# Four list tables, one for each block of tokens, in place of one in a mixture-of-experts encoder block

## The chip, the core and the metric

The kernel is one program on one core of a Trainium2 chip. Its time is the device time of one execution in microseconds (us). Five engines run their own instruction streams and meet at semaphores: TensorE (PE, matrix products; its loads of stationary operands are listed as PEld), VectorE (DVE), ScalarE (ACT), GpSimd (POOL) and SyncE (SP, which here only issues transfers). Sixteen DMA engines move data between the device memory and the on-chip memory; SP and POOL issue nearly all transfers.

## What is computed

A block of an encoder for 512 tokens of width 1024: a layer norm, a token mixer (gated linear attention and differential attention), a layer norm, a mixture of 32 experts of which every token uses 4, and a last layer norm. What matters here is how tokens come to experts:

```
logits = xf @ router_w + router_b          # 512 x 32
top_v, top_i = top_k(logits, 4)            # 4 experts of each token
gates = softmax(top_v)
...                                        # tokens grouped by expert
g = min(xe @ w_gate[e] + b_gate[e], 7);  u = clip(xe @ w_up[e] + b_up[e], -7, 7)
a = g * sigmoid(1.702 g) * (u + 1);      yb = a @ w_down[e] + b_down[e]
y[token] += yb * gate
```

Each expert has three matrices of 1024 x 1024 float32, 4 MB each, so the experts read 403 MB of weights.

## The kernel before

The first 700 us or so compute the mixer, with its weights streamed through a ring of buffers. Then come the experts, one after the other in `experts`. The loop step `e` computes gate and up of expert `e` (`gate_up`), then down of expert `e - 1` (`down`). Their weights arrive in pieces of 1 MB, two rows of 128 x 1024, into twelve buffers; `load` issues the next piece on SP's queue as soon as a buffer is given back. Experts 0 to 3 are computed in three float32r products (high and low parts; ACT makes `wh`, DVE makes `wl`), the rest are sorted by their number of tokens and most are computed in plain float32 in 32-column pieces (L1334).

Work on the side is put between the k steps of these products through hooks and generators. `order` (step 0, up, k = 6 until step 1) sorts the experts and at its end writes a table in device memory, `s_tab`: one row of 512 entries for each expert place, of which entry *n* says which (token, choice) is the *n*-th of that expert. A token chooses four experts, there are four blocks of 128 tokens, so this is sixteen scatters by indirect DMA from POOL (L1698), each writing 128 numbers of 4 bytes, one for each token of a block. Sixteen scatters write one tensor, and the framework makes each of them wait until the one before it has landed. After them POOL makes the small matrices `R` (L1703), scales a row block of `z` (L1513), gathers the rows of a later expert into `x` (L1215), and at the end of step 1 reads the first 160 columns of the table back into `tab` (L1517); then it scatters expert 0's result (L1223).

`lists` runs in step 2 between the k steps of gate: it transposes `tab` on PE (L1710, L1711), copies it on ACT (L1714, L1715), spreads it by small products (L1718 to L1721) and turns it into row numbers on DVE. These row numbers serve the gathers and scatters of the experts from 4 on. PE executes its instructions in the order in which they are written, so L1710 stands between the products of k = 0 and k = 1 of gate in step 2, and whatever it waits for stops these products as well.

Also in step 1, `plan_rest` (L1491) loads the sorted order of the 28 later experts into SP's registers, between two transfers of weights.

Of the kernel before, what the change touches and what calls it, by code (L numbers as in the profile page):

```python
# [5 lines left out]
F32 = mybir.dt.float32  # L6
# [8 lines left out]
P = 128  # L15
T = 512
NB = T // P
D = 1024
KC = D // P
E = 32  # L20
# [8 lines left out]
WIDE = 20  # L29
# [99 lines left out]
class Weights:  # L129
# [3 lines left out]
    def __init__(self, tc, ring, raw, ahead=2):  # L133
        self.tc, self.ring, self.raw, self.ahead = tc, ring, raw, ahead
        self.todo, self.raws, self.subs = [], {}, []
        self.n_raw = self.n_sub = self.n_out = 0
        self.low = tc.nc.vector
# [756 lines left out]
class Moe:  # L894
# [5 lines left out]
    def __init__(self, tc, K, a, z, gr):  # L900
        nc, c = tc.nc, K.c
        self.tc, self.nc, self.K, self.c, self.a, self.z = tc, nc, K, c, a, z
        self.rp = rp = K.open("route", "right")

        self.raw_r = K.open("rawr", "right")
        self.head = self.raw_r.tile([P, RAW_K, D], F32, tag=f"raw{RAW_R}", bufs=1, name="head")
        self.rw = rp.tile([P, KC, E], F32, name="rw")
        self.rb = rp.tile([P, 1, E], F32, name="rb")
        nc.sync.dma_start(self.rw, a["router_w"][0].rearrange("(k p) e -> p k e", p=P))
        nc.sync.dma_start(self.rb[:, 0], a["router_b"].broadcast_to([P, E]))  # L910
        self.hT, self.picks, self.gr = {}, {}, gr
        self.lg = rp.tile([P, NB, E], F32, name="lg")
        self.mx = rp.tile([P, NB, 8], F32, name="mx8")
        self.ix = rp.tile([P, NB, 8], U32, name="ix8")
        self.gates = rp.tile([P, NB, 4], F32, name="gates")

        self.prg = rp.tile([P, NB, 3, E], F32, name="prg")
        self.pm, self.rv, self.gv = (self.prg[:, :, i] for i in range(3))
        self.sel = rp.tile([P, NB, E], F32, name="sel")
        self.picks[0] = rp.tile([P, NB, P], F32, tag="pick0", bufs=1, name="pick0")  # L920

        self.srow, self.grow = (rp.tile([P, N_FIXED], I32, name=n) for n in ("srow", "grow"))
        self.srows, self.grows = (rp.tile([P, 5 * E + 1], I32, name=n) for n in ("srows", "grows"))
        self.tab = rp.tile([E, TAB], F32, name="tab")
        nc.gpsimd.memset(self.tab, 0.0)
        self.d_tab = K.d_tab.rearrange("(s r) o -> s (r o)", r=T)[:, :TAB]
        nc.gpsimd.dma_start(self.d_tab, self.tab)

        self.oh = rp.tile([P, E], F32R, name="oh")
        for i in range(0, P, E):  # L930
            nc.vector.tensor_copy(self.oh[i:i + E], c.ident[i:i + E, i:i + E])
        self.ohs = rp.tile([P, 2, E], F32R, name="ohs")
        self.spread(0, E)
        self.bias = rp.tile([P, 3, T], F32R, name="bias")
        self.bias_parts = []

        bts = self.head.rearrange("p r (n t) -> p (r n) t", t=T)
        for which, n in enumerate(("exp_b_gate", "exp_b_up", "exp_b_down")):
            bt = bts[:, which]
            for i in range(4):  # L940
                nc.sync.dma_start(bt[i * E:(i + 1) * E], a[n][0][:, (i // 2) * T:(i // 2 + 1) * T])

            def parts(bt=bt, which=which):
                bias = self.bias[:, which]
                if which == 1:
                    nc.vector.tensor_scalar(bt, bt, 1.0, None, op0=ALU.add)
                nc.scalar.copy(bias, bt)
                for lo in (E, 3 * E):
                    nc.vector.tensor_sub(bias[lo:lo + E], bt[lo:lo + E], bias[lo:lo + E].bitcast(F32))
            self.bias_parts.append(parts)  # L950

        self.todo, self.kinds, self.keep, self.raws, self.subs = [], [], [], {}, []
        self.n_sub = self.n_out = self.n_split = 0
        self.ohg = {}

        self.n_raw = self.spare = len(SPARE)
        self.sub_pool = None
        self.n_w = 3 * KC // RAW_K * E
        for i in range(N_FIXED):
            self.plan(i, [])  # L960
        own = [(self.raw_r, f"raw{i}", 1) for i in range(RAW_R + 1)]
        self.free = own[:-1] + [(K.raw, "raw", RAW_BUFS)] * RAW_BUFS + own[-1:]
        self.slots, self.held, self.want, self.due = {}, [], 0, []
# [453 lines left out]
    def experts(self, out):  # L1417
        nc, c, tc, a = self.nc, self.c, self.tc, self.a
# [30 lines left out]
        for e in range(E):  # L1449
# [6 lines left out]
            def first(which, k):  # L1456
# [22 lines left out]
                if e == 2 and which == 0:  # L1479
                    next(lists, None)  # L1480
# [19 lines left out]
            def middle(k):  # L1500
                nonlocal xT
                self.tick()
                if rest and k in (K_U2 if WIDE <= e < WIDE + 2 else K_U):
                    rest.pop(0)()
                if k in K_X and 0 < e < E - 1:
                    if k == K_X[0]:
                        xT = self.place("x", FORM[e + 1])
                    self.turn_part(x, xT, FORM[e + 1], K_X.index(k))
                if k == 6 and e == 0:
                    for j, n in enumerate(("ln2_g", "ln2_b")):  # L1510
                        nc.sync.dma_start(self.K.gb[:, j], a[n].broadcast_to([P, D]))
                if k == 3 and e < NB:
                    nc.gpsimd.tensor_scalar_mul(self.z[e], self.z[e], ALPHA)  # L1513
                if k == 7 and e + 1 < E and (FORM[e + 1] is not None or e + 1 == WIDE):
                    self.biases_of(e + 1, FORM[e + 1] or SECOND)
                if k == 7 and e == 1:
                    nc.gpsimd.dma_start(self.tab, self.d_tab)  # L1517
                if k == 5:
                    if e + 2 < E:
                        self.gather(x, e + 2, FORM[e + 2])  # L1520
                    if e + 2 == WIDE:
                        nc.gpsimd.memset(x2[0], 0.0)
                        self.gather(x2[0], E, SECOND)
                    if e + 3 == WIDE:
                        wide.append(self.held.pop())
                        t = self.other(wide[0], F32, "x2").rearrange("p i (n t) -> p (i n) t", t=T)
                        x2.extend(t[:, i] for i in range(4))
# [83 lines left out]
    def order(self):  # L1611
# [3 lines left out]
        nc, c, rp, lt = self.nc, self.c, self.rp, self.left  # L1615
# [37 lines left out]
        pt = self.psl()  # L1653
# [5 lines left out]
        pl = self.psl()  # L1659
# [7 lines left out]
        pt = self.psl()  # L1667
        for b in range(NB):
            nc.tensor.matmul(pt[:, b * 3 * E:(b + 1) * 3 * E], lhsT=tr[:3 * E, b * P:(b + 1) * P],
                             rhs=bd[:3 * E].rearrange("p i e -> p (i e)"), start=True, stop=True)  # L1670
# [4 lines left out]
        pl = self.psl()  # L1675
# [18 lines left out]
        to = rp.tile([P, NB, 4], I32, name="to")  # L1694
        with nc.allow_low_precision(reason="whole numbers below 2^24"):
            nc.vector.tensor_reduce(to, eq, axis=AX.X, op=ALU.add)
        for i in range(4 * NB):
            nc.gpsimd.indirect_dma_start(out=self.K.d_tab, out_offset=bass.IndirectOffsetOnAxis(ap=to[:, i // 4, i % 4:i % 4 + 1], axis=0),  # L1698
                                         in_=c.val[:, i:i + 1], in_offset=None, bounds_check=E * T - 1, oob_is_err=False)

        R = self.R = lt.tile([P, NB, P], F32, tag="pe", bufs=2, name="R")
        for i, (g, lo) in enumerate(((2, 0), (4, 0), (4, 32), (4, 64))):
# [3 lines left out]
    def lists(self):  # L1706

        nc, c, rp = self.nc, self.c, self.rp
        pt = self.psl()
        nc.tensor.transpose(pt[:, :E], self.tab[:, :P], c.ident[:E, :E])  # L1710
        nc.tensor.transpose(pt[:E, E:2 * E], self.tab[:, P:], c.ident[:E, :E])  # L1711
        yield
        lt = self.left.tile([P, 2, E], F32, name="lt")
        nc.scalar.copy(lt[:, 0], pt[:, :E])  # L1714
        nc.scalar.copy(lt[:E, 1], pt[:E, E:2 * E])  # L1715
        yield
        pl = self.psl()
        nc.tensor.matmul(pl[:, :E], lhsT=c.ident, rhs=lt[:, 0], start=True, stop=True)  # L1718
        for i in range(4):
            nc.tensor.matmul(pl[:, (i + 1) * E:(i + 2) * E], lhsT=self.R[:, i], rhs=lt[:, 0], start=True, stop=True)  # L1720
        nc.tensor.matmul(pl[:, 5 * E:5 * E + 1], lhsT=self.R[:E, 1], rhs=lt[:E, 1, WIDE:WIDE + 1], start=True, stop=True)  # L1721
        yield
        n = 5 * E + 1
        r = self.left.tile([P, D], F32, tag="y", bufs=1, name="r")
        t, r = r[:, :n], r[:, T:T + n]
# [8 lines left out]
        w, h, f = slice(0, E), slice(E, 2 * E), slice(2 * E, n)  # L1734
# [137 lines left out]
TAB = P + 32  # L1872
# [4 lines left out]
def build(tc, a, out):  # L1877
    nc = tc.nc
    K = Ctx()
    K.c = c = Ctx()  # L1880
    dr = lambda n, s: nc.dram_tensor(n, s, F32).ap()
# [10 lines left out]

    K.open, K.close = open_pool, close_pool
    K.d_h1 = dr("s_h1", (T, D))
    K.d_tab = dr("s_tab", (E * T, 1))
    for n in ("oT", "rg", "sA", "sB", "mA", "bT"):
        setattr(K, "d_" + n, dr("s_" + n, (KC, P, T)))
    with tc.tile_pool(name="cst", bufs=1) as cp, \
            tc.tile_pool(name="psB", bufs=4, space=PSUM) as psB, tc.tile_pool(name="psL", bufs=4, space=PSUM) as psL:
        K.psB, K.psL = psB, psL  # L1900
        tab = cp.tile([P, C_MIX], F32, name="tab")
# [81 lines left out]
```

## Time and profile before

| | |
|---|---|
| median of three runs | 1884.68 us (1884.49 to 1887.01) |
| the profiled execution | 1889.02 us, of which its span 1887.2 us |
| PE busy | 1754.7 us, 93% of the span |
| DVE, ACT, POOL busy | 763.7, 621.6, 462.6 us |
| bytes moved | 524.92 MB, mean 278 GB/s |
| longest wait of PE for a DMA | 44.5 us, once, at L1710 |

Times in the rows are from the start of the span. A row of the view of waits says which engine at which line and tile waited for whom, how long in total, how often, and the longest. In a timeline a row has its start, its length, engine, line, operation, output and inputs, and in brackets how long the engine was idle before and what ended that. A window row lists the busy time of each engine in a stretch (with its instructions in brackets), the granted clock of PE as a share of full speed, the share of the DMA engines' time that was busy, and GB/s.

### The profile page before, as it was taken

Reading aid. Unit: us, or ns where it says so; the run is one execution under the profiler, and the core shown is the slowest. Engines: PE = TensorE matmul, PEld = TensorE weight load, DVE = VectorE, ACT = ScalarE, POOL = GpSimd, SP = SyncE. Lnnn points to the kernel's source line nnn. Section 1 sums busy time; section 2 is a strip of 40 time slices with the busy share of each in tenths; the row PEclk is TensorE's granted clock in tenths of the full one; section 3 lists DMA queues with packets and bytes.
Section 4 is the critical chain, followed back from the end, with each engine's and each line's share of the span. In section 5 each row is a group of like instructions: output and inputs, shape, how many; then the busy total and the mean of one; then the engine's idle time right before and its main releaser. Section 6 shows DMA issues by size and latency. Waiting matters only on the chain. (4 is left out here: it accounts for less than half of the span.)

```text
span 1887.2 us, 33795 instructions
## 1 busy us (share of the span) xinstructions
PE 1754.7 (93%) x14065; PEld 1179.7 (63%) x14065; DVE 763.7 (40%) x1104; ACT 621.6 (33%) x997; POOL 462.6 (25%) x381
## 2 busy tenths in 40 slices
PE   7899999999999999918999999999999999997996
PEld 5687887777777888817655555555555455542573
DVE  5346658766753457927720000000002410000488
ACT  5433345555552234716621011110103311100473
POOL 4203316744432126231111111111102010101104
PEclk9998999999999998969999999999999999999998
DMA  7233432124335774736999999999999999999992
GB/s 244 90 100 103 154 101 89 53 78 161 113 129 205 269 287 161 272 156 248 350 405 377 420 371 423 380 417 390 401 376 413 366 380 423 424 424 426 426 426 95
DMA packets 111458, 524.92 MB, mean 278 GB/s; under 512 B 15390, under 2 KB 15734, under 8 KB 61508
## 3 DMA queue, kind: packets, MB, share of 16 engines
q1 hardware_dynamic: 97940, 492.05, 66.9%
q0 software_dynamic: 11056, 26.47, 3.7%
q10 hardware_dynamic: 2304, 4.20, 0.6%
q8 instruction: 112, 1.84, 0.4%
q14 instruction: 46, 0.38, 0.1%
HBM read 490.72 MB, written 37.91 MB: 280 GB/s over the span
## 5 line engine op out<-in xcount | busy, mean ns | idle before, releaser
L1334 PE MATMUL psb<-raw,xn 128*32 128x256 f32 (+1 forms) x5952 | 438.9, 404 | 12.3 <-DMA raw<-in_exp_w_up_dram 7.7
L1334 PEld LDWEIGHTS psb<-raw,xn 128*32 128x32 f32 (+1 forms) x5952 | 206.5, 113 | 199.9 <-issue 61.6
L1350 DVE TENSOR_SCALAR u<-psb 128x512 f32<-128x512 f32 (+1 forms) x52 | 31.5, 605 | 619.0 <-PE psb L1334 619.0
L1046 DVE TENSOR_TENSOR wl<-raw,wh 128x1024 fp32r<-128x1024 f32 x162 | 194.4, 1222 | 102.4 <-issue 50.3
L1334 PE MATMUL psl<-raw,an 128*32 128x256 f32 (+1 forms) x2976 | 226.1, 402 | 3.2 <-DMA raw<-in_exp_w_down_dram 2.2
L1035 ACT CAST wh<-raw 128x1024 fp32r<-128x1024 f32 x162 | 167.8, 1050 | 80.9 <-PE psb L1325 41.6
L1215 POOL DMA_INDIRECT x<-s_h,grows x55 | 59.7, 1085 | 472.3 <-PE psl L1261 411.3
L228 PE MATMUL psb<-hTh,wh 128*128 128x512 f32 x384 | 162.6, 423 | 8.8 <-ACT sg L543 3.9
L1334 PEld LDWEIGHTS psl<-raw,an 128*32 128x32 f32 (+1 forms) x2976 | 105.9, 112 | 91.4 <-issue 34.0
L230 PE MATMUL psb<-hTl,wh 128*128 128x512 f32 x384 | 154.2, 402 | 0.0
L229 PE MATMUL psb<-hTh,wl 128*128 128x512 f32 x384 | 154.1, 401 | 0.0
L168 ACT CAST wh<-raw 128x1024 fp32r<-128x1024 f32 x88 | 91.8, 1046 | 129.2 <-PE psb L230 81.0
L1223 POOL DMA_INDIRECT s_y<-y,srows x52 | 52.8, 1015 | 317.5 <-ACT y L1413 161.0
L1262 ACT COPY xn<-psl 128x512 f32<-128x512 f32 (+1 forms) x38 | 18.8, 495 | 310.3 <-PE psl L1261 310.3
L169 POOL TENSOR_TENSOR wl<-raw,wh 128x1024 fp32r<-128x1024 f32 x36 | 91.7, 2548 | 113.7 <-ACT wh L168 76.5
L169 DVE TENSOR_TENSOR wl<-raw,wh 128x1024 fp32r<-128x1024 f32 x52 | 68.2, 1315 | 93.4 <-ACT wh L168 93.4
L1326 PE MATMUL psb<-wl,xh 128*128 128x512 f32 x224 | 90.1, 402 | 4.6 <-DVE wl L1046 4.5
L1324 PE MATMUL psb<-wh,xh 128*128 128x512 f32 x224 | 93.1, 415 | 1.0 <-ACT wh L1035 1.0
L228 PEld LDWEIGHTS psb<-hTh,wh 128*128 128x128 f32 x384 | 74.0, 193 | 28.2 <-ACT sg L543 4.8
L1325 PE MATMUL psb<-wh,xl 128*128 128x512 f32 x224 | 89.4, 399 | 0.7 <-DVE xl L1285 0.7
L230 PEld LDWEIGHTS psb<-hTl,wh 128*128 128x128 f32 x384 | 73.7, 192 | 18.8 <-DVE hTl L348 0.9
L229 PEld LDWEIGHTS psb<-hTh,wl 128*128 128x128 f32 x384 | 74.0, 193 | 18.1 <-issue 2.2
(453 smaller groups left out, 2773.9 us busy)
## 6 DMA issues: line engine op xcount, KB each, us to landing
raw<-in_exp_w_up_dram SPq DMA_DIRECT2D x128, 1024.0 KB
raw<-in_exp_w_down_dram SPq DMA_DIRECT2D x128, 1024.0 KB
raw<-in_exp_w_gate_dram SPq DMA_DIRECT2D x125, 1024.0 KB
raw<-in_w_in_dram SPq DMA_DIRECT2D x32, 1024.0 KB
s_y<-zero SPq DMA_DIRECT2D x16, 512.0 KB
raw<-s_y SPq DMA_DIRECT2D x8, 1024.0 KB
raw<-in_w_br_gla_dram SPq DMA_DIRECT2D x4, 1024.0 KB
raw<-in_w_br_diff_dram SPq DMA_DIRECT2D x4, 1024.0 KB
```

The lines of the kernel that those rows point to most:

```text
L168: nc.scalar.copy(h, raw[:, 2 * s:2 * s + 2])
L169: self.low.tensor_sub(l, raw[:, 2 * s:2 * s + 2], h.bitcast(F32))
L228: nc.tensor.matmul(out, lhsT=sh, rhs=mh, start=first, stop=False)
L229: nc.tensor.matmul(out, lhsT=sl, rhs=mh, start=False, stop=False)
L230: nc.tensor.matmul(out, lhsT=sh, rhs=ml, start=False, stop=last)
L1035: nc.scalar.copy(h, src)
L1046: nc.vector.tensor_sub(sub[2], sub[0], sub[1].bitcast(F32))
L1215: self.nc.gpsimd.indirect_dma_start(out=x[:, t * D // n:(t + 1) * D // n], out_offset=None, in_=self.K.d_h1.rearrange("t (n d) -> (t n) d" ...
L1324: nc.tensor.matmul(ps[n], lhsT=xh[:, k], rhs=h[:, cs], start=False, stop=False)
L1325: nc.tensor.matmul(ps[n], lhsT=xl[:, k], rhs=h[:, cs], start=False, stop=False)
L1326: nc.tensor.matmul(ps[n], lhsT=xh[:, k], rhs=l[:, cs], start=False, stop=k == KC - 1)
L1334: nc.tensor.matmul(ps[t * d // T][i * m:i * m + m, t * d % T:t * d % T + d], lhsT=xT[:, o:o + m], rhs=w[:, i * d:(i + 1) * d], start=False ...
```

## The change

There are four tables in device memory, `s_tab0` to `s_tab3`, one for each block of 128 tokens, in place of one. All four are cleared early, from a corner of `prg` instead of `tab`. The scatters go around the blocks: choice 0 of blocks 0, 1, 2, 3, then choice 1, and so on. The read-back at the end of step 1 becomes eight loads: of each table the first 128 columns of all 32 rows (`tab`), and for the one wide expert's row the 32 columns behind (`ext`). In `lists` the sum of the four tables and its transposition are made by four products with the identity that add up in one PSUM tile, and a fifth sums `ext` with ones. The later products are the same, with the second part narrowed to one column.

```diff
-        self.tab = rp.tile([E, TAB], F32, name="tab")
-        nc.gpsimd.memset(self.tab, 0.0)
-        self.d_tab = K.d_tab.rearrange("(s r) o -> s (r o)", r=T)[:, :TAB]
-        nc.gpsimd.dma_start(self.d_tab, self.tab)
+        self.d_tabs = [t.rearrange("(s r) o -> s (r o)", r=T)[:, :TAB] for t in K.d_tabs]
+        none = self.prg.rearrange("p b i e -> p (b i e)")[:E, :TAB]
+        nc.gpsimd.memset(none, 0.0)
+        for t in self.d_tabs:
+            nc.gpsimd.dma_start(t, none)
...
                 if k == 7 and e == 1:
-                    nc.gpsimd.dma_start(self.tab, self.d_tab)
+                    self.tab = left.tile([P, NB, P], F32, tag="pe", bufs=2, name="tab")[:E]
+                    self.ext = left.tile([NB, TAB - P], F32, name="ext")
+                    for b, t in enumerate(self.d_tabs):
+                        nc.gpsimd.dma_start(self.tab[:, b], t[:, :P])
+                        nc.gpsimd.dma_start(self.ext[b:b + 1], t[WIDE:WIDE + 1, P:])
...
-        for i in range(4 * NB):
-            nc.gpsimd.indirect_dma_start(out=self.K.d_tab, out_offset=bass.IndirectOffsetOnAxis(ap=to[:, i // 4, i % 4:i % 4 + 1], axis=0),
-                                         in_=c.val[:, i:i + 1], in_offset=None, bounds_check=E * T - 1, oob_is_err=False)
+        for j in range(4):
+            for b in range(NB):
+                nc.gpsimd.indirect_dma_start(out=self.K.d_tabs[b], out_offset=bass.IndirectOffsetOnAxis(ap=to[:, b, j:j + 1], axis=0),
+                                             in_=c.val[:, 4 * b + j:4 * b + j + 1], in_offset=None, bounds_check=E * T - 1,
+                                             oob_is_err=False)
...
-        nc.tensor.transpose(pt[:, :E], self.tab[:, :P], c.ident[:E, :E])
-        nc.tensor.transpose(pt[:E, E:2 * E], self.tab[:, P:], c.ident[:E, :E])
+        for b in range(NB):
+            nc.tensor.matmul(pt[:, :E], lhsT=self.tab[:, b], rhs=c.ident[:E, :E], start=b == 0, stop=b == NB - 1)
+        nc.tensor.matmul(pt[:E, E:E + 1], lhsT=self.ext, rhs=c.ones[:NB, 0:1], start=True, stop=True)
         yield
-        lt = self.left.tile([P, 2, E], F32, name="lt")
-        nc.scalar.copy(lt[:, 0], pt[:, :E])
-        nc.scalar.copy(lt[:E, 1], pt[:E, E:2 * E])
+        lt = self.left.tile([P, E + 1], F32, name="lt")
+        nc.scalar.copy(lt[:, :E], pt[:, :E])
+        nc.scalar.copy(lt[:E, E:], pt[:E, E:E + 1])
...
-    K.d_tab = dr("s_tab", (E * T, 1))
+    K.d_tabs = [dr(f"s_tab{b}", (E * T, 1)) for b in range(NB)]
```

On POOL, at the end of `order` in step 1, the kernel before has these instructions in a row (`z0`, `z1` are row blocks of the residual, `s_h1` holds the normalized tokens, `to` the places to write, `li` the list of overfull experts, `x` the rows of the next expert, `y` a result):

```order
L1513 TENSOR_SCALAR z0_4743<-z0_4743 128x1024
L1215 DMA x_5681<-s_h1,grow_5065 128x1024
L1698 DMA s_tab<-tab_64,to_6063 16384x1 x16
L1703 COPY R_6113<-tab_64 128x128 x4
L1496 TENSOR_LOAD li_6037
L1513 TENSOR_SCALAR z1_4744<-z1_4744 128x1024
L1215 DMA x_5681<-s_h1,grow_5065 128x1024
L1517 DMA tab_5068<-s_tab 32x160
L1223 DMA s_y<-y_6633,srow_5064 2048x1024
```

In the changed kernel the scatters stand at the same place and begin like this:

```order
L1217 DMA x_5683<-s_h1,grow_5065 128x1024
L1705 DMA s_tab0<-tab_64,to_6065 16384x1
L1705 DMA s_tab1<-tab_64,to_6065 16384x1
L1705 DMA s_tab2<-tab_64,to_6065 16384x1
L1705 DMA s_tab3<-tab_64,to_6065 16384x1
L1705 DMA s_tab0<-tab_64,to_6065 16384x1
```

and behind the sixteen scatters and the four copies of `R` POOL has:

```order
L1515 TENSOR_SCALAR z1_4744<-z1_4744 128x1024
L1217 DMA x_5683<-s_h1,grow_5065 128x1024
L1522 DMA tab_6620<-s_tab0 32x128
L1523 DMA ext_6621<-s_tab0 1x16x2
L1522 DMA tab_6620<-s_tab1 32x128
L1523 DMA ext_6621<-s_tab1 1x16x2
L1522 DMA tab_6620<-s_tab2 32x128
L1523 DMA ext_6621<-s_tab2 1x16x2
L1522 DMA tab_6620<-s_tab3 32x128
L1523 DMA ext_6621<-s_tab3 1x16x2
L1225 DMA s_y<-y_6644,srow_5064 2048x1024
```

A scatter now has the one to the same table four instructions ahead of it, not one; all other instructions of POOL keep their order, with eight loads where one was. Beside the tensors that it touches, the framework gives POOL's transfers eight semaphores in rotation, so a transfer also waits until the eighth before it has landed; of the eight loads this adds a wait to the last one only, for the gather into `x` ahead of them.

On PE, the products of gate in step 2 (`wh`, `wl` are the parts of the weights, `xh`, `xl` those of the tokens) are interrupted by `lists` here, in the kernel before:

```order
L1325 MATMUL psb<-wh,xl 128x512
L1326 MATMUL psb<-wl,xh 128x512
L1710 MATMUL psl<-tab 128x32
L1711 MATMUL psl<-tab 32x32
L1324 MATMUL psb<-wh,xh 128x512
```

and in the changed kernel here:

```order
L1327 MATMUL psb<-wh,xl 128x512
L1328 MATMUL psb<-wl,xh 128x512
L1719 MATMUL psl<-tab 128x32 x4
L1720 MATMUL psl<-ones,ext 32x1
L1326 MATMUL psb<-wh,xh 128x512
```

The place among the products is the same; the two transpositions, which waited for one load, are five small products, which wait for eight.

## Rows read from the trace of the kernel before

**Rows 1.** The page's first part: busy us, share of the span, instructions.
```profile
PE 1754.7 (93%) x14065; PEld 1179.7 (63%) x14065; DVE 763.7 (40%) x1104; ACT 621.6 (33%) x997; POOL 462.6 (25%) x381
```

**Rows 2.** Waits of all engines: who for whom, us in total, times, longest.
```profile
PE psl L1710 <- DMA tab<-s_tab: 44.5, 1, 44.5
POOL s_tab L1698 <- DMA s_tab<-tab,to: 44.0, 15, 5.6
```

**Rows 3.** Windows: busy PE, PEld, DVE, ACT, POOL; clock; DMA share; GB/s.
```profile
784.00:812.00 28.00, 25.95 (x116) 20.59 (x114) 26.67 (x27) 21.37 (x24) 9.28 (x7) 1.00 0.49 177
812.00:854.00 42.00, 0.00 (x0) 0.00 (x0) 0.62 (x1) 0.00 (x0) 16.23 (x18) 0.52 0.41 162
854.00:858.00 4.00, 3.48 (x10) 2.74 (x11) 0.19 (x1) 0.93 (x3) 1.82 (x1) 0.50 0.06 24
1000.00:1600.00 600.00, 599.21 (x7592) 320.33 (x7590) 66.62 (x90) 90.30 (x166) 81.58 (x80) 1.00 0.98 395
```

**Rows 4.** Timeline of PE around its longest wait.
```profile
809.65 0.39 PE L1326 MATMUL psb<-wl,xh 128*128 128x512 f32 x1
...
854.52 0.28 PE L1710 MATMUL psl<-tab 32*128 32x32 f32 x1 [44.48 <-DMA tab<-s_tab]
```

**Rows 5.** Timeline of POOL: scatters 1, 2, 3, 8, 9, 16 and what follows.
```profile
783.77 1.75 POOL L1698 DMA_INDIRECT s_tab<-tab,to  x1 [10.46 <-DVE to L1696]
787.60 1.90 POOL L1698 DMA_INDIRECT s_tab<-tab,to  x1 [2.08 <-DMA s_tab<-tab,to]
794.49 0.97 POOL L1698 DMA_INDIRECT s_tab<-tab,to  x1 [5.00 <-DMA s_tab<-tab,to]
...
815.45 0.97 POOL L1698 DMA_INDIRECT s_tab<-tab,to  x1 [5.58 <-DMA s_tab<-tab,to]
821.69 0.98 POOL L1698 DMA_INDIRECT s_tab<-tab,to  x1 [5.27 <-DMA s_tab<-tab,to]
...
845.04 0.98 POOL L1698 DMA_INDIRECT s_tab<-tab,to  x1 [1.91 <-DMA s_tab<-tab,to]
846.02 0.99 POOL L1703 COPY R<-tab 128x128 f32<-128x128 f32 x4
...
849.94 1.09 POOL L1215 DMA_INDIRECT x<-s_h,grow  x1 [0.18 <-issue]
851.04 0.59 POOL L1517 DMA_DIRECT2D tab<-s_tab  x1
```

**Rows 6.** Groups of POOL's instructions, 783 to 812: busy us, mean ns.
```profile
L1698 POOL DMA_INDIRECT s_tab<-tab,to x7 | 9.5, 1358 | 27.1 <-DMA s_tab<-tab,to 16.6 <-DVE to L1696 10.5
```

**Rows 7.** Timeline of POOL, 921 to 926: gathers of one expert.
```profile
921.61 1.54 POOL L1215 DMA_INDIRECT x<-s_h,grows  x1 [23.03 <-PE psl L1261]
923.46 1.50 POOL L1215 DMA_INDIRECT x<-s_h,grows  x1 [0.31 <-issue]
```

**Rows 8.** The gathers' line, 840 to 1000: issue to landing.
```profile
DMA to landing us min/median/max: 5.8/6.1/6.4
```

**Rows 9.** Timeline of DVE, 784 to 812: its longest stretch without a pause.
```profile
785.13 11.95 DVE L1046 TENSOR_TENSOR wl<-raw,wh 128x1024 fp32r<-128x1024 f32 x10
```

**Rows 10.** Timelines of SP's queue: loads of weights around the wait.
```profile
808.80 2.11 SPq L1012 DMA_DIRECT2D raw<-in_exp_w_down_dram  x4
811.01 1.97 SPq L1012 DMA_DIRECT2D raw<-in_exp_w_gate_dram  x2
...
860.72 0.33 SPq L1012 DMA_DIRECT2D raw<-in_exp_w_gate_dram  x1
```

**Rows 11.** Waits of SP's queue, 1000 to 1200, then 1600 to 1800.
```profile
SPq L1012 <- PE psb L1334: 104.2, 49, 3.2
...
SPq L1012 <- DMA raw<-in_exp_w_gate_dram: 51.3, 24, 3.1
```

**Rows 12.** Timeline of POOL: the clearing of the table, and what follows it.
```profile
667.11 0.54 POOL L927 DMA_DIRECT2D s_tab<-tab  x1 [0.29 <-DMA head<-in_exp_b_up_dram]
702.57 2.40 POOL L1087 TENSOR_TENSOR z<-z,gb 128x1024 f32<-128x1024 f32 x1 [34.92 <-issue]
```

More of the change, by code (lines that the diff above doesn't have):

```diff
@@ L1709, in lists @@
         pt = self.psl()
-        nc.tensor.transpose(pt[:, :E], self.tab[:, :P], c.ident[:E, :E])
-        nc.tensor.transpose(pt[:E, E:2 * E], self.tab[:, P:], c.ident[:E, :E])
+        for b in range(NB):
+            nc.tensor.matmul(pt[:, :E], lhsT=self.tab[:, b], rhs=c.ident[:E, :E], start=b == 0, stop=b == NB - 1)
+        nc.tensor.matmul(pt[:E, E:E + 1], lhsT=self.ext, rhs=c.ones[:NB, 0:1], start=True, stop=True)
         yield
-        lt = self.left.tile([P, 2, E], F32, name="lt")
-        nc.scalar.copy(lt[:, 0], pt[:, :E])
-        nc.scalar.copy(lt[:E, 1], pt[:E, E:2 * E])
+        lt = self.left.tile([P, E + 1], F32, name="lt")
+        nc.scalar.copy(lt[:, :E], pt[:, :E])
+        nc.scalar.copy(lt[:E, E:], pt[:E, E:E + 1])
         yield
         pl = self.psl()
-        nc.tensor.matmul(pl[:, :E], lhsT=c.ident, rhs=lt[:, 0], start=True, stop=True)
+        nc.tensor.matmul(pl[:, :E], lhsT=c.ident, rhs=lt[:, :E], start=True, stop=True)
         for i in range(4):
-            nc.tensor.matmul(pl[:, (i + 1) * E:(i + 2) * E], lhsT=self.R[:, i], rhs=lt[:, 0], start=True, stop=True)
-        nc.tensor.matmul(pl[:, 5 * E:5 * E + 1], lhsT=self.R[:E, 1], rhs=lt[:E, 1, WIDE:WIDE + 1], start=True, stop=True)
+            nc.tensor.matmul(pl[:, (i + 1) * E:(i + 2) * E], lhsT=self.R[:, i], rhs=lt[:, :E], start=True, stop=True)
+        nc.tensor.matmul(pl[:, 5 * E:5 * E + 1], lhsT=self.R[:E, 1], rhs=lt[:E, E:], start=True, stop=True)
         yield
```

## The prediction

> **What bounds the kernel now.** The page's first part comes first [rows 1]: PE is busy for 93% of the span, so the question is what it waits for in the rest, and whether the change touches that. The chain of waits that the page gives covers only the last microseconds here, so I went to the waits of all engines [rows 2]. The reader should see two rows of almost equal size: PE waits once, for 44.5 us, for the load of `tab`, and POOL waits 15 times, 44.0 us together, for its own scatters into `s_tab`. The windows [rows 3] show what the first of these means: between 812 and 854 PE, DVE and ACT do nothing, and only POOL works.. The timelines say how the two rows hang together. PE's last product before the wait starts at 809.65 and the transposition at 854.52 [rows 4]. POOL's first scatter starts at 783.77 and the sixteenth at 845.04 [rows 5]. That is 61.27 us for 15 steps, or 4.08 us a step, while one scatter keeps POOL itself for 0.97 to 1.90 us. The rest of each step is the wait for the scatter before to land. Then come 5.02 us of other POOL work (846.02 to 851.04) and the load, 3.48 us from its start to PE's restart.
>
> So in this stretch a chain of sixteen small writes, one behind the other, sets the time, and everything else stands behind it. Is PE's restart also what sets the end? From 1000 to 1600 PE is busy 599 of 600 us [rows 3], and SP's queue holds its loads back for buffers that PE gives free [rows 11]; between 1600 and 1800 the loads wait for one another. A PE that is earlier gives its buffers free earlier, so the stream of weights moves with it.
>
> **The change, part by part.** *Pace of the scatters.* A scatter now waits for the one four ahead. Two costs of a step remain: POOL's own time and the gap to its next transfer. While DVE and ACT work (the first seven scatters) a scatter takes 1.36 us in the mean [rows 6], afterwards 0.97 or 0.98 [rows 5]. The gap between two transfers on POOL that don't wait for each other is 0.30 us, seen in the gathers of a later expert [rows 7]. All sixteen now fall in the busy stretch, so I take 1.36 + 0.30 = 1.66 us a step. The same table comes round after 4 x 1.66 = 6.6 us, and the steps of before, which contain a full landing, were at most 6.89 us (787.60 to 794.49) and 4.08 in the mean. The wait for the landing is thus all but covered by the three scatters to other tables. The sixteenth ends at 783.77 + 16 x 1.36 + 15 x 0.30 = 810.0, where it was 846.02.
>
> *From there to PE's restart.* The copies of `R`, the scaling of `z` and the gather keep their 5.02 us, so the first load starts at 815.1. Eight loads at 0.59 us put the start of the eighth at 819.2, but it also waits for the gather, which starts 1.1 us before the first load, at 814.0, and lands 6.1 us later [rows 8], at 820.1. From the start of a load to PE it was 3.48 us with almost idle DMA engines. At 820 they are not idle: six loads of weights go out between 808.80 and 813 [rows 10], right behind one that started just before. At 162 GB/s with the DMA engines 41% busy [rows 3], near 395 GB/s when they are busy, these seven pieces, 7.3 MB, need 18.6 us, until about 827. In that same stretch a scatter took 6.24 us from start to start of the next (815.45 to 821.69). Between 3.48 and 6.24 I take 5.0. PE restarts at 825.1, 29.4 us before 854.52.
>
> *Costs on PE.* Five small products for two, taken as 0.1 us each, at the half clock that PE is granted after such a pause (0.50 in rows 3, the 1.2 GHz level, over 42 us without a product): 0.3 us more. The clock itself changes nothing: its mean over the pause is 0.52 and over the 4 us behind it 0.50, so it falls early in the pause and rises soon after it, and a pause of 15 us should have both. Net 29.1 us.
>
> *What costs nothing.* Three more clears of tables, at 0.54 us each, stand on POOL at 667, ahead of a pause of 34.92 us [rows 12]. The memory they are cleared from is now `prg`, so DVE's first write of `prg` waits for them; it comes with the logits of the first block, behind that pause. ACT's two copies are of the same number and no larger. Behind the eight loads POOL has expert 0's scatter, a scaling of `z` and the gather for expert 4; the gather waits for PE anyway, and all three now start earlier than in the kernel before.
>
> *Both ends.* Early: every scatter at 0.97 + 0.30, the sixteenth ends at 803.8, the gather lands 5.8 us after 807.7, the last load starts there and takes 3.48: PE restarts at 817.0, 37.2 us earlier after PE's 0.3. Late: every scatter at 1.90, the sixteenth ends at 783.77 + 30.4 + 4.5 = 818.7, the gather lands 6.4 us after 822.6, the last load takes 6.89: 835.9, 18.3 us earlier. I stay with the middle, since the mean of seven scatters in the very same stretch is the nearest row.
>
> *The sum.* The profiled execution took 1889.02 us, 1.8 us of it outside its span; less 29.1 that is 1859.9. The median of the runs was 4.34 us lower than the profiled one, 1884.68, and the stall is of the same program, so I take the same 29.1 from it: 1855.6 us.
>
> **A rule that speaks against it.** The second and third scatters of before lie wholly beside DVE's longest stretch without a pause, 785.13 to 797.08 [rows 9], and took 1.90 and 0.97 us: POOL is slowed there, not stopped. The Trainium skill, "SBUF — State Buffer", section "SBUF: two separate sides", says that while DVE runs certain instructions POOL cannot write the descriptors of its DMAs, and gives 620 ns alone against 3100 ns beside DVE. By that figure sixteen scatters would be an estimated 54 us, and almost all of the gain would be gone. The same page, "Who interferes with whom", exempts the two-input kind of instruction that fills this stretch, and the two rows agree with that. The first rival below is what its strong form would do here.
>
> **The rivals.**
> 1. *POOL makes its descriptors only when DVE pauses.* Then up to DVE's last instruction, near 812.6, no more scatters get out than before, which is seven [rows 6], and the other nine follow at 1.27 us: the sixteenth ends at 824.0, the gather lands at 834.0, the last load, now with idle DMA engines, is at PE at 837.5. Gain 16.7 us, 1868.0. For it: scatters of 1.90 and 1.75 us in the busy stretch. Against it: one of 0.97 in the middle of it. Chance 0.09.
> 2. *PE restarts early but meets weights that have not landed.* Now all buffers are full long before 854.52; in the forecast the last of the seven pieces lands at about 827.4, after PE's restart. If PE needed that piece at once it would stand until then: 2.3 us less, a gain of 26.8 us, 1857.9. For it: the loads wait for one another after 1600 [rows 11], so the stream has no room there to make up for a loss. Against it: the pieces land in the order in which they are used, gate and up of expert 2 were issued before the seven or with the first of them, and SP's next load, held back until a buffer was free, went out only at 860.72, 6.2 us after the restart [rows 10]. Chance 0.10.
> 3. *Slower: the scatters go one at a time whatever table they write.* If the 4.08 us of a step are the time that POOL's transfer queue takes for 128 writes of 4 bytes, and not a wait that the tables impose, then the sixteenth still ends at 846.02, and the seven more loads are added behind it: the gather lands at 849.94 + 6.1 = 856.0, the eighth load starts then and reaches PE at 859.5. That is 5.0 us later than now, with PE's 0.3 us 5.3 us slower: 1890.0. This side is reached where a step stays above (846.02 - 5.3 - 0.98 - 783.77) / 15 = 3.73 us. For it: the trace shows no two scatters to different tensors in a row, so it doesn't tell the two readings apart by itself. Against it: two gathers of far more bytes start 1.85 us apart on the same queue, while a gather lands only after 5.8 to 6.4 us [rows 7, 8], so transfers do overlap there. It is also the case in which the change doesn't do what it says. Chance 0.06.
>
> **How the numbers follow.** The forecast, 1855.6 us, has a chance of 0.75. Its bounds are 37.2 and 18.3 us of gain, which is 1847.5 to 1866.4; they contain the second rival and end just short of the first. The range of 1846 to 1867 leaves out half of the first rival, all of the third, and a little for what I have not thought of. A measurement of this kernel tells about 0.2%, 3.8 us, from no change. Every case but the third is far beyond that: faster 0.94, and of the third's 0.06 a third falls within 0.2%: same 0.02, slower 0.04.
>
> **What would show it.** In the changed profile: the sixteen scatters at steps of 1.3 to 2.2 us and a wait of POOL for `s_tab` of a few us in place of 44.0 (the first step of the sum); the first load of `tab` near 815 and the eighth near 820; one wait of PE at L1719 or L1720 of some 15 us in place of 44.5; the same clock of 0.5 for a few us after it; the rows from 1000 on shifted by the same 29 us, with PE as busy as before. It would be wrong if the scatters kept steps near 4 us, if single scatters took 3 us beside DVE, or if PE's restart were near 825 and PE then waited for weights somewhere behind it.

## The result, and the profile after

The changed kernel takes 1865.13 us, the median of 4 runs (1862.65 to 1871.66), against 1885.59 us (1884.49 to 1887.01) for the kernel before in the same session. The ratio is 0.9896, with a 95% interval of 0.9869 to 0.9924: 20.5 us are gained where 29.1 were forecast, and the forecast time was 1855.6 us. The profiled execution took 1866.6 us, its span 1864.7 us; the granted clock over it is 0.975, where it was 0.966.

The waits come first, as they did before [rows 2]. Each row says who waited for whom, us in total, times, and the longest.

```profile
PE psl L1719 <- DMA tab<-s_tab: 19.2, 4, 17.3
...
POOL s_tab L1705 <- DMA s_tab<-tab,to: 2.0, 2, 1.1
```

POOL's 44.0 us of waiting for its own scatters have become 2.0. PE's wait of 44.5 us has become 19.2 in four pieces, not one of 15 or so as forecast. The timeline of POOL shows where the stage now spends its time [rows 5].

```profile
786.66 1.75 POOL L1705 DMA_INDIRECT s_tab<-tab,to  x1 [10.45 <-DVE to L1702]
788.71 1.40 POOL L1705 DMA_INDIRECT s_tab<-tab,to  x1 [0.30 <-issue]
790.42 1.95 POOL L1705 DMA_INDIRECT s_tab<-tab,to  x1 [0.30 <-issue]
...
797.20 0.98 POOL L1705 DMA_INDIRECT s_tab<-tab,to  x1 [0.30 <-issue]
...
800.64 0.98 POOL L1705 DMA_INDIRECT s_tab<-tab,to  x1 [1.13 <-DMA s_tab<-tab,to]
802.44 1.65 POOL L1705 DMA_INDIRECT s_tab<-tab,to  x1 [0.82 <-DMA s_tab<-tab,to]
...
814.41 2.00 POOL L1705 DMA_INDIRECT s_tab<-tab,to  x1 [0.30 <-issue]
816.41 0.99 POOL L1711 COPY R<-tab 128x128 f32<-128x128 f32 x4
...
820.33 1.09 POOL L1217 DMA_INDIRECT x<-s_h,grow  x1 [0.18 <-issue]
821.43 0.60 POOL L1522 DMA_DIRECT2D tab<-s_tab  x1
...
824.47 0.54 POOL L1522 DMA_DIRECT2D tab<-s_tab  x1
829.70 0.50 POOL L1523 DMA_DIRECT2D ext<-s_tab  x1 [4.69 <-DMA x<-s_h,grow]
```

The reader should see three things. Most brackets of the scatters now hold only the 0.30 us of a gap between transfers, and two hold a short wait for the scatter four ahead. The sixteenth ends at 816.41, 29.75 us after the first one starts, where that took 62.25 us [rows 5]. And the last load waits: it starts at 829.70, when the gather of 820.33 has landed, 9.37 us later. The group of the scatters' line from 780 to 817, with its mean in ns, and the landings of `tab` and `ext` (from issue; minimum, median, maximum; of the eighth load no landing is recorded) give the sizes:

```profile
L1705 POOL DMA_INDIRECT s_tab<-tab,to x16 | 23.8, 1490 | 16.4 <-DVE to L1702 10.5 <-issue 3.7 <-DMA s_tab<-tab,to 2.0
```

```profile
DMA to landing us min/median/max: 8.8/9.1/9.5
...
DMA to landing us min/median/max: 8.8/9.2/9.3
```

On PE the tables' products stand between 830.32 and 834.93, and the products of gate go on at 834.86 [rows 4]:

```profile
830.32 0.60 PE L1719 MATMUL psl<-tab 32*128 32x32 f32 x2 [17.35 <-DMA tab<-s_tab]
...
834.04 0.63 PE L1719 MATMUL psl<-tab 32*128 32x32 f32 x2 [0.74 <-DMA tab<-s_tab]
834.67 0.26 PE L1720 MATMUL psl<-ones,ext 4*32 4x1 f32 x2
834.86 0.80 PE L1326 MATMUL psb<-wh,xh 128*128 128x512 f32 x1
```

PE's last wait, at 834.04, is for the fourth load of `tab`. It went out at 824.47 without a wait and took 9.5 us to land. The product that reads `ext` comes right behind, without an idle time that the trace shows, so the eighth load had landed by about 834.67.

The windows (busy PE, PEld, DVE, ACT, POOL; clock; DMA share; GB/s) answer to [rows 3]:

```profile
812.00:854.00 42.00, 22.79 (x98) 18.55 (x97) 17.35 (x28) 13.56 (x20) 16.55 (x19) 0.72 0.71 260
...
820.00:830.00 10.00, 0.00 (x0) 0.00 (x0) 0.00 (x0) 0.00 (x0) 5.12 (x10) 0.50 1.00 380
854.00:858.00 4.00, 4.00 (x19) 3.32 (x18) 3.60 (x4) 3.07 (x4) 0.00 (x0) 1.00 1.00 377
...
1000.00:1600.00 600.00, 600.00 (x7577) 317.71 (x7573) 65.84 (x88) 91.80 (x169) 86.82 (x85) 1.00 0.99 398
```

Between 820 and 830, while the loads of the tables are under way, the DMA engines are fully busy. In the kernel before they were 41% busy over the whole pause [rows 3], but that is a mean of two halves. When its one load ran, from 851 on, they were nearly idle:

```profile
830.00:854.00 24.00, 0.00 (x0) 0.00 (x0) 0.00 (x0) 0.00 (x0) 13.30 (x15) 0.50 0.06 15
```

So the small loads of the changed kernel meet a stream of weights that the load of before had not met.

### The profile page after: what moved, and what is told of

It is laid out like the page before. It is cut to its first block, busy times and chain, and to the rows that moved or that the text cites. A ratio compares the mean times of both kernels' runs of the same rounds, so it can differ in the third digit from the quotient of the medians.

```text
span 1864.7 us, 33825 instructions
## 1 busy us (share of the span) xinstructions
PE 1748.9 (94%) x14073; PEld 1170.9 (63%) x14073; DVE 766.1 (41%) x1104; ACT 621.6 (33%) x997; POOL 474.0 (25%) x391
## 5 line engine op out<-in xcount | busy, mean ns | idle before, releaser
L1336 PE MATMUL psb<-raw,xn 128*32 128x256 f32 (+1 forms) x5952 | 440.9, 405 | 13.2 <-DMA raw<-in_exp_w_gate_dram 6.9
L1336 PEld LDWEIGHTS psb<-raw,xn 128*32 128x32 f32 (+1 forms) x5952 | 206.8, 113 | 201.9 <-issue 61.4
L1336 PE MATMUL psl<-raw,an 128*32 128x256 f32 (+1 forms) x2976 | 221.8, 402 | 2.5 <-DMA raw<-in_exp_w_down_dram 2.4
L1336 PEld LDWEIGHTS psl<-raw,an 128*32 128x32 f32 (+1 forms) x2976 | 101.7, 112 | 90.9 <-issue 27.0
```

The costliest lines, as they stand in the source:

```text
L1336: nc.tensor.matmul(ps[t * d // T][i * m:i * m + m, t * d % T:t * d % T + d], lhsT=xT[:, o:o + m], rhs=w[:, i * d:(i + 1) * d], start=False ...
```

## The experiments

All edits are against the changed kernel. The lengths in the table are counted from the start of the first scatter, since that moment itself lay anywhere from 782.70 to 788.46 us in ten profiles, although only the clears differ ahead of it. "Restart" is the first product of gate behind the tables' products on PE; *lists later* and *loads at once* have no such wait any more.

| kernel | first scatter | 16th ends after | restart after | ratio to before | 95% interval |
|---|---|---|---|---|---|
| before | 783.77 | 62.25 | 71.02 | 1 | |
| before, again | 784.15 | 61.88 | 70.71 | | |
| changed | 786.66 | 29.75 | 48.20 | 0.9896 | 0.9869 to 0.9924 |
| changed, again | 784.61 | 29.72 | 48.11 | 0.9886 | 0.9864 to 0.9908 |
| loads first | 783.77 | 29.73 | 43.77 | 0.9872 | 0.9855 to 0.9888 |
| blockwise | 788.46 | 57.10 | 67.82 | 1.0 | 0.9986 to 1.0014 |
| weights held | 784.73 | 29.72 | 40.60 | 0.9854 | 0.9838 to 0.9871 |
| two tables | 782.70 | 42.50 | 52.30 | 0.9928 | 0.9904 to 0.9953 |
| lists later | 786.20 | 29.74 | | 0.9792 | 0.9776 to 0.9809 |
| loads at once | 784.53 | 29.72 | | 0.9789 | 0.9776 to 0.9803 |

### Loads first: the gather behind the loads, not ahead of them

```diff
-                if k == 7 and e == 1:
+                if k == 5 and e == 1:
                     self.tab = left.tile([P, NB, P], F32, tag="pe", bufs=2, name="tab")[:E]
```

> The eight loads of the tables stand ahead of the 512 KB gather on POOL, not behind it; nothing else moves. In the changed kernel a load took 8.8 to 9.5 us to land and PE restarted 48.2 us after the first scatter. Theory A (the weights that fill the DMA engines make every transfer late): the loads still take about 9 us, start 1.1 us earlier and the last one no longer waits for the gather; PE restarts about 46 us after the first scatter, 1863 us. Theory B (the gather's bytes stand ahead of the loads on POOL's own queue): the loads take 5 to 6.5 us, PE restarts 41 to 43 us after the first scatter, 1858 to 1860 us.

It took 1862.7 us, the median of 4 runs (1858.33 to 1865.03). The eight loads go out from 817.21 to 820.79 without a wait; of PE's wait and of the landings of `tab` and `ext` the trace says:

```profile
PE psl L1719 <- DMA tab<-s_tab: 14.7, 4, 12.6
...
DMA to landing us min/median/max: 5.3/6.0/6.3
...
DMA to landing us min/median/max: 5.7/6.1/6.5
```

Without the gather ahead of them the loads land in 6.0 us, not in 9.1, and PE restarts 4.4 us sooner after the first scatter. So beside the weights the gather accounts for 3.1 us of a landing, and the other 6.0 us are there without it. The landing is that of theory B; the restart, 43.77 us, lies between the two theories, and the time is the 1863 us of theory A.

### Weights held: no pieces of weights beside the loads

SP's queue lets 28 pieces of weights go and holds back the rest; a small transfer of `ext` on that queue makes it wait until the loads of `ext`, the last of the eight among them, have landed.

```diff
-        while self.n_raw < n and self.free:
+        while self.n_raw < n and self.free and (self.go or self.n_raw < 28):
...
+                    nc.sync.dma_start(self.K.d_null, self.ext)
+                    self.go = True
+                    self.load()
```

> The changed kernel, but SP's queue holds the loads of weights from the first piece of down of expert 1 on until the table's loads have landed (a small transfer on SP that reads ext stands ahead of them). The DMA engines are then nearly free of weights while the gather and the eight loads run. Theory A (weights): the gather lands in about 5 us and the loads in 3.5 to 5, PE restarts 41 to 43 us after the first scatter, 1858 to 1861 us if PE doesn't lack the held weights later. Theory B (gather ahead on the same queue): landings stay at 8 to 9 us, restart at 47 to 48 us, 1864 to 1866 us.

It took 1859.96 us, the median of 4 runs (1857.59 to 1860.58). The gather is ahead of the loads as in the changed kernel (818.38, the loads from 819.48). The rows are the last load, PE's wait, the landings of `tab` and `ext`, and the window 812 to 830.

```profile
823.01 0.53 POOL L1523 DMA_DIRECT2D ext<-s_tab  x1
...
PE psl L1722 <- DMA tab<-s_tab: 12.1, 1, 12.1
...
DMA to landing us min/median/max: 2.0/2.5/3.5
...
DMA to landing us min/median/max: 1.7/2.2/3.1
...
812.00:830.00 18.00, 6.87 (x27) 5.87 (x28) 3.01 (x4) 1.76 (x4) 14.90 (x18) 0.62 0.41 146
```

With the DMA engines 41% busy instead of full, the loads land in 2.5 us although the gather is ahead of them. The gather itself has landed before the last load is issued, within 4.6 us, and the last load doesn't wait. PE restarts 7.6 us sooner after the first scatter than in the changed kernel. This is theory A's outcome, a little beyond its sizes. Together the two experiments fill a table of four:

| landing of a load of `tab`, median | gather ahead | no gather ahead |
|---|---|---|
| weights streaming | 9.1 us (changed) | 6.0 us (loads first) |
| no weights | 2.5 us (weights held) | not run |

Two theories of the landing stood against each other in what was expected, the gather ahead in POOL's queue and the weights in the DMA engines, and each was right in half. Beside weights a load takes 6.0 us with no gather ahead of it, more than the 2.5 us behind a gather without weights. Beside weights the 512 KB of the gather cost 3.1 us more. What they cost without weights can't be said, since the fourth kernel was not run: in weights held the first load, issued at 819.48, took 3.5 us, and so landed just behind the gather, which took 4.4 us from 818.38; the last load of `tab`, issued 3 us later, took 2.0 us. Why the weights and the gather add up was not shown.

### Blockwise: four tables, written one after the other

```diff
-        for j in range(4):
-            for b in range(NB):
+        for b in range(NB):
+            for j in range(4):
```

> Four tables as in the change, but all four scatters of a block one after the other, so 12 of 15 scatters again follow one to the same table. If the wait for the same table is what set the pace before: 12 steps of about 4.1 to 4.5 us and 3 of 1.85, the sixteenth scatter starts some 56 to 60 us after the first (27.8 in the changed kernel, 61.3 before), PE restarts 68 to 72 us after the first (70.8 before), 1883 to 1888 us. Rival (the gain came from other tables or other places in memory, not from the order): steps near 1.85, 1865 us.

It took 1887.38 us, the median of 10 runs (1884.22 to 1893.18), no different from before. The rows are POOL's waits for its scatters, the last scatter, and the landing of the loads of `tab`.

```profile
POOL s_tab L1705 <- DMA s_tab<-tab,to: 37.5, 12, 5.5
...
844.59 0.98 POOL L1705 DMA_INDIRECT s_tab<-tab,to  x1 [1.48 <-DMA s_tab<-tab,to]
...
DMA to landing us min/median/max: 1.8/2.5/3.5
```

Twelve waits remain, those inside a block; the three steps from one block to the next have only the gap of 0.30 us. All else of the change is in this kernel, so the four tables gain nothing without the new order of the scatters. Nor is a cost of the eight loads or the five products seen, as far as this can tell: the restart comes 3.2 us sooner after the first scatter than before, and no time is gained. The landing of 2.5 us (median, of `tab`) is a second case of loads behind a gather with few weights in the way: from 830 to 854 the DMA engines are 22% busy.

### Two tables

Two blocks share a table; there are two loads of each kind and three products.

```diff
-    K.d_tabs = [dr(f"s_tab{b}", (E * T, 1)) for b in range(NB)]
+    K.d_tabs = [dr(f"s_tab{b}", (E * T, 1)) for b in range(2)]
...
-                nc.gpsimd.indirect_dma_start(out=self.K.d_tabs[b], ...
+                nc.gpsimd.indirect_dma_start(out=self.K.d_tabs[b % 2], ...
```

> Two tables, each for two blocks, so a scatter waits for the one two ahead, and four loads. If a step is the larger of POOL's own 1.8 us and the landing (4.1 us in the mean, 6 to 7 with full DMA engines) divided by the number of tables: steps of 2.0 to 3.3 us, the sixteenth starts 32 to 42 us after the first (27.8 with four tables, 61.3 with one). The weights have landed some 43 us after the first scatter, so the gather and the loads run with emptier DMA engines and take less than the 9 us of the changed kernel; PE restarts 46 to 54 us after the first scatter (48.2 with four): 1864 to 1871 us. Rival (each table's chain is paced by something other than its landing): steps of 4 us, 1885 us.

It took 1871.65 us, the median of 4 runs (1866.42 to 1878.65), just above what was expected; the restart, 52.30 us, is inside. POOL's waits and its last scatter:

```profile
POOL s_tab L1705 <- DMA s_tab<-tab,to: 20.1, 10, 4.9
...
824.22 0.98 POOL L1705 DMA_INDIRECT s_tab<-tab,to  x1 [1.13 <-DMA s_tab<-tab,to]
```

From the first start to the sixteenth the scatters take 61.3 us with one table, 41.5 with two and 27.8 with four, that is 4.08, 2.77 and 1.85 us a step. With four tables 2.0 us of waits are left, so more tables could take no more than that from the scatters.

### Lists later, with the loads first: work for PE while it waits

Beside the earlier loads, `lists` is moved from the steps of gate in step 2 to those of up.

```diff
-                if e == 2 and which == 0:
+                if e == 2 and which == 1 and k >= 2:
                     next(lists, None)
```

> The loads ahead of the gather as in the run before, and the products that use them moved on PE from gate of expert 2 to up of expert 2, from its third row on: PE comes to them some 17 us later. If the wait for the tables is the only thing that PE lacks there: the wait falls from 17.3 us to under 3, PE's clock doesn't fall, 1841 to 1847 us. Rival (without the pause the stream of weights falls behind and PE waits for weights instead): the 20 us come back as waits of PE for raw, 1855 us or more.

It took 1849.23 us, the median of 4 runs (1847.01 to 1850.2). That is 13.5 us less than loads first alone, but 2 us more than the upper end of what was expected. The rows are the tables' first product on PE, up's next one behind them, and the window from 830.

```profile
827.58 0.40 PE L1719 MATMUL psl<-tab 32*128 32x32 f32 x2
...
831.96 0.80 PE L1326 MATMUL psb<-wh,xh 128*128 128x512 f32 x1
...
830.00:854.00 24.00, 22.36 (x95) 17.99 (x96) 14.30 (x25) 11.76 (x15) 5.12 (x3) 0.86 1.00 397
```

The long wait is gone, but the products of the tables still come a little ahead of their loads, three of the four after waits of 0.53 to 0.83 us, 2.0 us together, and the granted clock falls to 0.86 for this stretch.

### Loads at once: the version that the experiments point to

The loads go out right behind the last scatter and the copies of `R`, ahead of the scaling of `z`, and `lists` starts one k step later. The edit is against lists later.

```diff
-                if e == 2 and which == 1 and k >= 2:
+                if e == 2 and which == 1 and k >= 3:
...
-                if k == 5 and e == 1:
+                if k == 2 and e == 1:
                     self.tab = left.tile([P, NB, P], F32, tag="pe", bufs=2, name="tab")[:E]
```

> As the run with the later lists, with the eight loads directly behind the copies of R, ahead of the scaling of z (2.8 us) and the gather, and the lists' products one row later still in up of expert 2. There PE waited 4.5 us for the tables and its clock was 0.86 over 24 us, some 3 us more. If that wait is what was left: no wait of PE at the tables, clock near 1.00 there, 1840 to 1845 us. Rival (the stream of weights is the bound by now, since it no longer runs ahead in a pause): 1847 to 1850 us, with more waits of PE for raw.

It took 1847.63 us, the median of 5 runs (1844.09 to 1849.1), the lowest of all, though above the range that was expected and where the rival had put it. The 4.5 us that the expectation names as a wait were the whole stretch of the tables' products in lists later, from 827.58 to 831.96; the waits in it were 2.0 us. Here PE meets its tables without a wait, at full clock:

```profile
827.26 1.07 PE L1719 MATMUL psl<-tab 32*128 32x32 f32 x8
828.26 0.22 PE L1720 MATMUL psl<-ones,ext 4*32 4x1 f32 x2
...
830.00:854.00 24.00, 22.27 (x105) 17.82 (x104) 18.77 (x30) 15.78 (x18) 2.54 (x2) 1.00 1.02 419
```

It is not measurably faster than lists later, since both intervals reach from 0.9776 to beyond 0.98. PE was already busy 22.36 of the 24 us there and is busy 22.27 here, with the DMA engines full in both: what is left in this stretch is no longer the tables. That the stream of weights is the bound by now is not shown: PE's waits for gate's and up's weights at L1336 are 15.5 us, and lie between 12.2 and 16.1 us in the other nine profiles.

### The kernel before, and the changed one, again

> The kernel before once more, for a second profile: when the first scatter starts (783.77 us in the first) and how long it takes from there to the end (1103.4 us), which tells how far single profiles of the same code differ. Both theories expect the same: the first scatter between 783 and 789 us, PE restarts 70 to 72 us after it.

The kernel before took 1882.94 us in its one run. PE's wait is that of the first profile, and the restart lies 0.3 us from it:

```profile
PE psl L1710 <- DMA tab<-s_tab: 44.2, 1, 44.2
```

Its span is 1881.1 us where the first profile's was 1887.2. The same code, at the same moment in this stage, differs by 6 us in what comes later. So a difference of a few microseconds behind the restart can't be read from two profiles.

> The changed kernel again, unaltered. If its restart of TensorE is set by the steps read in its first profile, the 16th scatter ends about 29.8 us after the first one starts, the gather lands about 9 us after its start and the main products restart about 48 us after the first scatter; the moment of the first scatter itself may lie anywhere from 782 to 789 us, as it did for kernels that share the code up to it, and the median should lie at 1861 to 1867 us. If the 9 us landing was one execution's accident, the restart comes at about 45 us and the median at 1859 to 1862 us.

The changed kernel took 1872.61 us, the median of 5 runs (1868.02 to 1874.54), above both ranges that were expected, on a chip where the kernel before took 1894.22 us; the ratio agrees with the first one, and the restart of 48.11 us is that of the first profile. The rows are the scatters' group and the last load of `ext`:

```profile
L1705 POOL DMA_INDIRECT s_tab<-tab,to x16 | 23.9, 1497 | 16.2 <-DVE to L1702 10.5 <-issue 3.7 <-DMA s_tab<-tab,to 1.8
...
827.43 0.50 POOL L1523 DMA_DIRECT2D ext<-s_tab  x1 [4.49 <-DMA x<-s_h,grow]
```

The gather starts at 818.25 here and lands 9.2 us later. PE's last wait is again for the fourth load of `tab`, issued at 822.40, and ends at 831.90. The terms that were missed have the same sizes as in the first profile, so they are no accident of one execution.

## Why the prediction was right, and where it was not

The measured 1865.13 us lie in the range of 1846 to 1867, near its upper end, and 2.9 us from the 1868.0 of the first rival; the time alone would not have told the two apart, the timeline of POOL does.

**What bounded the kernel was read rightly.** The chain of sixteen scatters set PE's restart, and PE's restart set the end. Blockwise has every part of the change but the order around the blocks, and gains nothing. Across the kernels with a restart, the time follows it: from blockwise to the changed kernel the restart comes 19.6 us sooner and the ratio falls by 0.0104, of 1886 us 19.6 us; weights held is 7.6 us sooner than the changed kernel and 0.0042 lower, 7.9 us.

**The first term, the pace of the scatters, was too small by 3.5 us.** The text took 1.36 us for a scatter and 0.30 for a gap, 26.3 us for all. Measured are 29.75 us: the mean scatter is 1.49 us, which makes 2.1 us more, and the wait for the scatter four ahead, "all but covered", makes gaps of 1.13 and 0.82 us out of two of 0.30, 1.35 us more. The mean of 1.36 was that of the first seven scatters of before [rows 6]; in the changed kernel the first seven have 1.57 and the other nine 1.42.

**The step that failed most is the landing of transfers beside the weights.** The prediction's sum lets PE wait for the eighth load alone, behind the gather. One term of it, the gather, was too small, and the landing of the seven loads ahead of the eighth did not stand in it. "It also waits for the gather, which ... lands 6.1 us later" became 9.4 us, 3.3 us more. The 6.1 us of [rows 8] are those of later gathers, in transfers of another size and with other work beside them. This gather moves 512 KB, at the moment when the weights fill the DMA engines; with weights held it landed within 4.6 us. The prediction saw the weights, and put a surcharge on the eighth load for them ("between 3.48 and 6.24 I take 5.0"; from 829.70 to PE at 834.67 it took at most 4.97), but none on the gather ahead of it. The load that PE waited for last, by the trace, is another: the fourth of `tab`, which waited for nothing on POOL and took 9.5 us, nearly twice that 5.0. So two paths end within 0.7 us of each other: had the last load not waited for the gather at all, PE would still have stood until 834.04 for `tab`. How the miss divides between them is therefore open.

The stretch from the end of the scatters to the gather was right to the hundredth, 3.92 us in both kernels. The forecast of 29.1 us less puts the restart 41.92 us after the first scatter (71.02 in the kernel before). It came after 48.20 us, 6.3 us later: 3.5 us of that are the pace of the scatters, and the other 2.8 us arise behind the gather's start, on these two paths. That the time still fell in the range is partly luck. The gather's 9.4 and the 9.5 of a load lie beyond even the late end of 6.4 and 6.89 us; the scatters, 29.75 us, stayed well short of their late end of 34.9, and that made up for it.

**"The stream of weights moves with it" was nearly right.** From the kernel before to the changed one the restart comes 22.8 us sooner, and the ratios make 19.6 and 21.5 us of that. In loads first and weights held they make 24.1 of 27.3 us, and 27.5 of 30.4; in blockwise, nothing of 3.2. The loss is 1 to 5 us each time; the intervals of these kernels just include no loss at all, but that of blockwise and that of two tables (13.6 of 18.7 us) exclude it by little. Between 1600 and 1800 the DMA engines are full in both kernels (share 1.01). SP's queue waits there for its own transfers for 154.9 us, where it was 133.5 (the sum of the three rows to which the last of [rows 11] belongs), and hardly for PE:

```profile
SPq L1014 <- DMA raw<-in_exp_w_down_dram: 54.1, 28, 2.2
SPq L1014 <- DMA raw<-in_exp_w_gate_dram: 53.0, 24, 3.0
SPq L1014 <- DMA raw<-in_exp_w_up_dram: 47.8, 24, 2.3
```

A lead that PE brings into a stretch in which the transfers set the pace can be lost in part. That the loss lies there is argued and not shown. The second profiles have 147.0 and 139.5 us in these rows, a difference of 7.5 us and not 21.4. And from the restart to the end of the span the two profiles of before take 1032 and 1026 us, the six others with a restart 1029 to 1035, so no loss behind the restart stands out. Part of it can lie ahead of the first scatter, which came at 786.66 us in the first profile of the changed kernel, 2.9 us later than before; that this is the clears is not shown either, since loads first and the second profile, with the same clears, have 783.77 and 784.61.

**The rivals.** POOL held up by DVE: the sixteen scatters went out while DVE worked, none longer than 2.01 us in any run, so the first rival did not happen. The Trainium skill's figure of 3100 ns for descriptors beside DVE ("SBUF — State Buffer", "SBUF: two separate sides") is not seen here, and the page's exemption of two-input instructions from that stall ("Who interferes with whom") agrees with these rows. PE at weights that have not landed: between 834 and 880 no wait of PE is for weights, and over the whole span its waits at L1336 for gate and up are 13.1 us in the changed kernel (6.9 and 6.2), and were 12.2 (4.5 and 7.7), so the second rival is not seen, though weights in flight did cost what the prediction missed, at the tables and not at PE. Scatters one at a time whatever they write: refuted by 1.85 us a step, and by the two-table kernel in between.

**The costs put at nothing** are not seen: blockwise carries them all and is level with before, within 0.14%, or 2.6 us. The clock behaved as forecast: 0.50 in the pause and up to 839.7, 1.00 from there to 854.

## What to carry to other kernels

A run of small writes to one tensor, each waiting for the one before it, is worth splitting into tensors and dealing out in turn: the step fell from 4.08 to 1.85 us, and splitting without dealing out in turn gained nothing. When a stall is shortened, look at what the DMA engines will be doing at the new moment, and take the landing of every transfer on the path from a row with that load, the one queued ahead as well. And put work between the start of a transfer and its reader: moving the reader from gate to up gave 13.5 us more than loads first alone, where the two ways of making the loads land sooner gave 4.5 us (loads first) and 7.9 us (weights held) by the ratios.

## What the runs showed of the hardware that was not expected

- The landing of a 16 KB load was 2.5 us behind a gather with no weights, 6.0 us beside weights, and 9.1 us with both: beside weights a gather ahead in the queue cost 3.1 us. The Trainium skill, "DMA: Bandwidth & Descriptors", section "Latency and other measured facts", has a smaller fixed cost under a lighter load; the direction agrees with these runs, and the sizes are theirs.
- A scatter takes 0.98 us or 1.95 us of POOL within one stretch in which DVE doesn't pause (790.42 and 797.20 above), and the same scatter of the sixteen has the same length, within 0.03 us, in the first and the second profile of the changed kernel, but for the ninth (1.65 and 1.78). What decides it was not found.
- Four small copies on POOL (`R`) took 0.99 us in the changed kernel and 3.15 us in the two kernels that keep PE and DVE at work beside them.
